# The meta tokens' attention gathered by key head, and four changes of order and engine at the borders of stages, in a two-layer attention and mLSTM trunk

## The chip, the cores and the metric

The kernel runs on one core of a Trainium2 chip, as one launch. A core has TensorE (PE, matrix products, with a weight load PEld of its own), VectorE (DVE), ScalarE (ACT), GpSimd (POOL) and SyncE (SP), which here only issues DMAs. The metric is the device time of one execution in microseconds (us), the median of several runs.

## The reference

Two layers; each normalises the rows, projects them once, runs two mixers side by side, gates both and projects back onto the residual. Sixteen learned meta rows stand ahead of the 1024 rows of x, and are dropped at the end. The first mixer is attention with 16 query heads on 2 key heads (8 query heads for each), a window of 128, the 16 meta keys always visible, and a sink logit for each head. The second is an mLSTM with 4 heads.

```python
h = concatenate([meta, x])                                   # 16 + 1024 rows of 1024
for l in range(2):
    z = rms_norm(h, norm_g) @ w_in
    aq, ak, av, ag, mq, mk, mv, mi, mf, mo, mgate = split(z)
    q, k = rope(rms_norm(aq, q_norm_g)), rope(rms_norm(ak, k_norm_g))
    # scores against 16 meta keys and the last 128 keys; the sink is one more term of the sum
    m = maximum(scores.max(-1), sink)
    e = exp(scores - m)
    probs = e / (e.sum(-1) + exp(sink - m))
    ya = (probs @ v) * silu(ag)
    qk = silu(causal_depthwise_conv(concatenate([mq, mk])))
    hm = rms_norm(mlstm(qk, mv, log_i, log_f), out_norm_g)
    ym = hm * sigmoid(mo) * silu(mgate)
    h = h + concatenate([ya, ym]) @ w_out
return h[16:]
```

A meta row's query sees only the meta keys that are not behind it, and the sink. Only layer 0 needs the outputs of the meta rows; in layer 1 they are dropped.

## The kernel before

All tensors are kept in float32. A product is made of two or three passes with each factor split into a rounded part (hi) and the rest (lo): ACT copies hi, then DVE or POOL subtracts. Rows are tiles t = 0 (the 16 meta rows) and t = 1 to 8 (128 rows each).

A layer runs as these stages: norm and key/value projection (`kv_tasks`), the first query projection (`q_tasks`), the attention over eight head pairs j, the mLSTM over four heads, and the output projection in four groups g (half of the tiles by half of the columns). `weave` interleaves a foreground list, the projection for a later stage, with a background list, the steps of attention or mLSTM. The matmuls stand on PE in the order of this code (`pin`); the instructions of the other engines are put in order by a scheduler that goes by readiness and priority, and `tc.high_priority(offset=EARLY)` moves some forward.

*Attention.* `att_tasks` gives, for a head pair j (two query heads, key head kv = j // 4), one step for each row tile b, in four parts that the background runs two and three steps apart. `s1`: the scores of tile b into bank S (L692), mask, maximum, exponentials, normalisation; in some steps ("visits") transposed queries ride in S's free columns (L633). `s2`: the probabilities are transposed into bank T (L738 for the 16 meta keys, L741 for the window), and evacuated to `HL` (L745, L748) and `pm` (L746, L749). `s3` and `s4`: the products with the values into bank O (L766, L778), evacuated by L781 and L783, multiplied by the gate G on POOL (L785) and stored to `spool` by SP. There are two S banks, one T and one O. In layer 0 b runs from 0 to 8 (`first_q` = 0), so each head pair has a ninth step, b = 0, with 16 query rows; its queries are turned by `q_meta` (L646) one head pair ahead. In layer 1 b runs from 1 to 8.

*Before the attention,* `q_tasks(0)` is the foreground. At its places n0+6 and n0+15 the keys of key head 0 are turned and stacked: `k_turn`, `k_stacks` (hi on ACT L444, lo on DVE L445) and `v_stacks` (ACT L452, POOL L453), for the first and the second half of the rows. `q_stacks` (L625, L610) turns the first queries.

*Elsewhere:* `fold` (L201, L202) adds the two halves of the product of the 16 meta rows. In the mLSTM, `sb` makes the factor of the output norm for each head and tile, 68 in all: DVE L1025 to L1029, a power on POOL (L1030), a DVE product (L1031), scaling on ACT (L1033), then a transpose on PE (L957). In the output projection `wout` splits a weight block on ACT (L185) and on POOL or DVE (L186), `y_split` splits a mixer's output (L1217, L1222), `product` is L1260, and `result` adds the residual (L1276, L1277) and takes squares (L1286). In group g = 2 of layer 0 the next layer's norm runs along: `norm_pre` (L291 to L295) and `norm_half` (L303 transposes, L307, L308).

Of the kernel before, what the change touches and what calls it, by code (L numbers as in the profile page):

```python
# [23 lines left out]
NEG = -1e30  # L24
# [12 lines left out]
WHEN = {0: (3, 4, 5, 6), 3: (2, 3, 4, 5), 4: (3, 4, 6, 7)}  # L37
FIRST = ((0, 0), (0, 1), (1, 0))


def _tables():
# [10 lines left out]
    cst = np.zeros((128, 166), f)  # L52
    cst[:, 0:128] = np.eye(128, dtype=f)
    cst[:, 128:164] = -0.5
    for r in range(64):
        cst[r, 164 + r // 16 % 2] = 1.0
    return {
# [7 lines left out]
def build(ctx, tc, I, O):  # L65
# [112 lines left out]
    def wout(l, k, c0, i, after=None):  # L178
# [7 lines left out]
        (ve if i > 8 and i % 2 else gp).tensor_tensor(lo, raw, hi, op=ALU.subtract)  # L186
# [11 lines left out]
    def fold(ps, n):  # L198

        a = w1k()  # L200
        sc.activation(a[:16, :n], ps[32:48, :n], AF.Copy)  # L201
        ve.tensor_tensor(a[:16, :n], ps[:16, :n], a[:16, :n], op=ALU.add)  # L202
        return a
# [169 lines left out]
    for l in range(DEPTH):  # L373
# [5 lines left out]
        AV = unit(F32R)[:, 0:896].rearrange("p (t c) -> p t c", t=7)  # L379
        DV = unit(F32R)[:, 0:896].rearrange("p (t c) -> p t c", t=7)  # L380
# [3 lines left out]
        KT = unit()[:, :].rearrange("p (a c) -> p a c", a=8)  # L384
        SS = []
# [87 lines left out]
        def kv_tasks():  # L473
# [13 lines left out]
            if l == 0:  # L487
# [4 lines left out]
                sy.dma_start(cst, I["cst"])  # L492
# [151 lines left out]
        def q_meta_turn(j, ps):  # L644
            c0 = 128 * (j % 2)
            pin(pe.transpose(ps, A[j]["q"]["XM"][:, c0:c0 + 128], ident[:16, :16]))  # L646
# [30 lines left out]
        def att_tasks(j, st):  # L677
# [3 lines left out]
            def s1(b):  # L681
# [21 lines left out]
                if b == 0:  # L703
                    ve.memset(band[:p], NEG)
                    mk = mask[:p, 128:144].bitcast(U32).rearrange("p (a c) -> p a c", a=1).to_broadcast([p, 2, 16])
                    ve.copy_predicated(cols(S, 130, 510, 16)[:p], mk,
                                       neg[:p].rearrange("p (a c) -> p a c", a=1).to_broadcast([p, 2, 16]))
# [18 lines left out]
                if meta:  # L726
                    q_put(q_unit(j + 1, 0)[:, 1024:1056], S[:, 0, 384:400], 16)
                live[b] = P

            def s2(b):  # L730
# [3 lines left out]
                HL = OW = None  # L734
# [4 lines left out]
                if b > 0:  # L739
                    for h in range(2):  # L740
# [626 lines left out]
```

## Time and profile before

| what | value |
|---|---|
| time, median of 3 runs (lowest to highest) | 1934.89 us (1934.46 to 1937.74) |
| the profiled execution | 1933.47 us |
| its span in the trace | 1931.7 us |
| granted TensorE clock | 1.00 |

The profile is one execution. Its rows give start, duration, engine, line, output <- input, shape; a number in square brackets is the idle time before the instruction and what ended it. A group's row has its count, then, behind a bar, the busy time of the engine in that group (overlaps counted once) and the mean duration of one instruction. The window rows give the window, its length, then busy time and count for PE, PEld, DVE, ACT and POOL, the granted clock, the DMAs' share and GB/s. A matmul's shape is contraction rows * output rows, then output rows x columns.

### The profile page before, as it was taken

Reading aid. Unit: us, or ns where it says so; the run is one execution under the profiler, and the core shown is the slowest. Engines: PE = TensorE matmul, PEld = TensorE weight load, DVE = VectorE, ACT = ScalarE, POOL = GpSimd, SP = SyncE. Lnnn points to the kernel's source line nnn. Section 1 sums busy time; section 2 is a strip of 40 time slices with the busy share of each in tenths; the row PEclk is TensorE's granted clock in tenths of the full one; section 3 lists DMA queues with packets and bytes.
Section 4 is the critical chain, followed back from the end, with each engine's and each line's share of the span. In section 5 each row is a group of like instructions: output and inputs, shape, how many; then the busy total and the mean of one; then the engine's idle time right before and its main releaser. Section 6 shows DMA issues by size and latency. Waiting matters only on the chain.

```text
span 1931.7 us, 36274 instructions
## 1 busy us (share of the span) xinstructions
PE 1902.6 (98%) x12827; PEld 1796.5 (93%) x12827; DVE 1051.2 (54%) x2914; ACT 1065.0 (55%) x3193; POOL 988.7 (51%) x1278
## 2 busy tenths in 40 slices
PE   8999999999999999999999999999999999999999
PEld 7999999999999999977789999999999999998887
DVE  7666766667354453542545667666573635437211
ACT  6577777746454554643334778776564545446221
POOL 3665756346545454564325467564465543647332
PEclk9999999999999999999999999999999999999999
DMA  4111111121222121554541111112122121216543
GB/s 155 32 45 40 38 44 43 45 65 41 64 54 59 43 62 50 154 170 159 176 134 36 44 48 38 49 48 60 40 59 64 47 71 41 62 59 195 167 148 125
DMA packets 150839, 148.28 MB, mean 77 GB/s; under 512 B 15081, under 2 KB 123921, under 8 KB 150658
## 3 DMA queue, kind: packets, MB, share of 16 engines
q1 hardware_dynamic: 150658, 145.97, 25.8%
q8 instruction: 101, 1.65, 0.4%
q14 instruction: 80, 0.66, 0.1%
HBM read 122.58 MB, written 23.29 MB: 76 GB/s over the span
## 4 chain that ended last, share of the span: by engine, by line
PE 82%; DVE 5%; ACT 3%; DMA 3%; POOL 3%; issue 2%; SPq 0%; ACTq 0%; POOLq 0%; DVEq 0%
PE pj L194 32%; PE pj L234 19%; PE pss L1260 6%; PE pj L1260 5%; PE po L1260 4%; PE S L692 3%; PE O L778 3%; PE po L957 2%; PE pss L957 2%; PE O L766 2%; PE T L741 1%; DMA raw<-in_w_out_dram 1%; DVE t L903 1%; PE pt L957 1%; PE pj L218 1%
## 5 line engine op out<-in xcount | busy, mean ns | idle before, releaser
L194 PE MATMUL pj<-H,RING 128*128 128x384 f32 (+2 forms) x3312 | 559.3, 322 | 0.0
L194 PEld LDWEIGHTS pj<-H,RING 128*128 128x128 f32 x3312 | 521.5, 188 | 2.3 <-issue 0.2
L168 POOL TENSOR_TENSOR RING<-raw,RING 128x512 fp32r<-128x512 f32 (+1 forms) x192 | 256.8, 1343 | 107.3 <-ACT RING L167 100.3
L234 PE MATMUL pj<-RING,H 128*128 128x256 f32 (+1 forms) x1920 | 268.8, 286 | 0.0
L234 PEld LDWEIGHTS pj<-RING,H 128*128 128x128 f32 x1920 | 242.2, 189 | 0.5
L234 PE MATMUL pj<-H,RING 128*128 128x384 f32 (+2 forms) x1296 | 239.7, 325 | 0.0
L186 POOL TENSOR_TENSOR RING<-raw,RING 128x512 fp32r<-128x512 f32 x96 | 126.1, 1320 | 172.8 <-ACT RING L185 159.7
L194 PE MATMUL pj<-RING,H 128*128 128x256 f32 x1536 | 209.6, 287 | 4.0 <-DVE w1k L202 2.1
L234 PEld LDWEIGHTS pj<-H,RING 128*128 128x128 f32 x1296 | 200.9, 188 | 0.1
L194 PEld LDWEIGHTS pj<-RING,H 128*128 128x128 f32 x1536 | 193.7, 191 | 6.5 <-DVE w1k L202 2.5
L185 ACT ACTIVATE RING<-raw 128x512 fp32r<-128x512 f32 x128 | 80.6, 631 | 174.8 <-DMA raw<-in_w_out_dram 155.4
L167 ACT ACTIVATE RING<-raw 128x512 fp32r<-128x512 f32 (+1 forms) x196 | 122.2, 625 | 47.0 <-DMA raw<-in_w_in_dram 35.2
L970 POOL TENSOR_TENSOR p<-u,p 128x258 fp32r<-128x258 f32 x64 | 49.5, 774 | 172.9 <-ACT p L969 164.9
L718 ACT ACTIVATE t<-S,mx 128x145 f32<-128x145 f32 (+1 forms) x272 | 99.4, 368 | 43.9 <-DVE mx L715 35.3
L785 POOL TENSOR_TENSOR u<-u,w1k 128x128 f32<-128x128 f32 (+1 forms) x136 | 61.9, 455 | 118.0 <-DVE w1k L783 102.2
L1260 PE MATMUL pss<-RING,H 128*128 128x512 f32 x384 | 120.5, 394 | 0.0
L756 POOL TENSOR_SCALAR_AFFINE_SELECT p<-p 128x512 fp32r<-128x512 f32 x112 | 71.4, 637 | 86.7 <-DVE p L748 85.7
L1260 PE MATMUL pj<-RING,H 128*128 128x512 f32 x352 | 110.3, 395 | 0.0
L903 DVE SCALAR_TENSOR_TENSOR t<-u,cw,t 128x384 f32<-128x384 f32 (+1 forms) x144 | 107.6, 747 | 2.0
L723 ACT ACTIVATE t<-t,mx 128x144 f32<-128x144 f32 (+1 forms) x272 | 97.7, 407 | 7.1 <-DVE mx L720 6.5
L926 DVE SCALAR_TENSOR_TENSOR t<-t,pj 128x384 f32<-128x384 f32 (+2 forms) x48 | 24.5, 511 | 124.9 <-ACT t L925 124.9
L1260 PE MATMUL po<-RING,H 128*128 128x512 f32 x288 | 91.3, 398 | 0.0
(347 smaller groups left out, 3841.3 us busy)
## 6 DMA issues: line engine op xcount, KB each, us to landing
raw<-in_w_out_dram SPq DMA_DIRECT2D x128, 256.0 KB, 2.8
raw<-in_w_in_dram SPq DMA_DIRECT2D x100, 256.0 KB, 2.8
raw<-in_w_in_dram SPq DMA_DIRECT2D x192, 128.0 KB, 2.3
spool<-u SPq DMA_DIRECT2D x56, 192.0 KB, 1.9
p<-x SPq DMA_DIRECT2D x24, 256.0 KB, 4.2
t<-spool SPq DMA_DIRECT2D x30, 192.0 KB, 3.6
p<-spool SPq DMA_DIRECT2D x26, 192.0 KB, 3.6
u<-em SPq DMA_DIRECT2D x8, 576.0 KB, 6.6
```

What stands on the lines that cost most here:

```text
L167: sc.activation(hi, raw[:, :, 0:o], AF.Copy)
L168: eng.tensor_tensor(lo, raw[:, :, 0:o], hi, op=ALU.subtract)
L185: sc.activation(hi, raw, AF.Copy)
L186: (ve if i > 8 and i % 2 else gp).tensor_tensor(lo, raw, hi, op=ALU.subtract)
L194: last = pin(pe.matmul(out, a, b, start=(i == 0), stop=(i == n - 1)))
L234: pin(pe.matmul(out(), x, y, start=(k + i == 0), stop=(k == n - 1 and i == 2)))
L718: sc.activation(P[:p, 145 * h:145 * h + 145], S[:p, h, 1 + 127 * h:146 + 127 * h], AF.Exp, bias=mx[:p, 0, h:h + 1], accum_out=mx[:p, 1, h: ...
L723: sc.activation(Pn, Pn, AF.Copy, scale=mx[:p, 2, h:h + 1])
L756: gp.affine_select(OW, HL, [[0, 4], [1, 128]], ALU.is_ge, 0.0, base=0, channel_multiplier=-1)
L903: ve.scalar_tensor_tensor(z, RAW[:, t0 + i:t0 + i + n], wcol(i), z, ALU.mult, ALU.add)
L957: pin(f(*a, **k))
L1260: pin(pe.matmul(ps[:p, :], a, b, start=(i + n == 0), stop=(i == 15 and n == len(terms) - 1)))
```

## The change

Five things are changed.

1. The meta queries' attention. The steps b = 0 of layer 0 are gone. The 16 queries of all eight heads of one key head are stacked to 128 columns (`QM`), and the steps named in `MRIDE`, b = 4 of j = 3 and of j = 7, carry them along: two score matmuls into free columns of S, `meta_probs`, one more transpose into T, one product into free columns of O, and `meta_out`, which multiplies by the gate's first 16 columns (kept in `GM`) and stores to `spool`. The queries are turned before the stage and in step b = 6 of j = 1, 3 and 5. `meta_consts` loads the mask and the sinks by nine small DMAs in the first head pair.
2. `fold`'s two operations get the higher priority.
3. `k_stacks` and `v_stacks` of the second half of the rows are called in the first head pair of the attention, not at n0+15.
4. In `sb` the product after the power goes from DVE to POOL; the constant factor is multiplied in by a DVE operation ahead of the power.
5. In group g = 2 of layer 0's output projection all weight splits go to DVE; before, they alternated between POOL and DVE from the ninth on.

```diff
+MRIDE = ((3, 4), (7, 4))
...
-    def wout(l, k, c0, i, after=None):
+    def wout(l, k, c0, i, after=None, eng=None):
...
-        (ve if i > 8 and i % 2 else gp).tensor_tensor(lo, raw, hi, op=ALU.subtract)
+        (eng or (ve if i > 8 and i % 2 else gp)).tensor_tensor(lo, raw, hi, op=ALU.subtract)
...
     def fold(ps, n):
 
         a = w1k()
-        sc.activation(a[:16, :n], ps[32:48, :n], AF.Copy)
-        ve.tensor_tensor(a[:16, :n], ps[:16, :n], a[:16, :n], op=ALU.add)
+        with tc.high_priority(offset=EARLY):
+            sc.activation(a[:16, :n], ps[32:48, :n], AF.Copy)
+            ve.tensor_tensor(a[:16, :n], ps[:16, :n], a[:16, :n], op=ALU.add)
         return a
...
+        AV, DV = unit(F32R), unit(F32R)
+        QMF, pmm = AV[:, 896:1152], DV[:, 896:1024]
+        QM = QMF.rearrange("p (v a h t) -> p v h a t", v=2, a=4, h=2)
+        AV, DV = [x[:, 0:896].rearrange("p (t c) -> p t c", t=7) for x in (AV, DV)]
...
-        def q_meta_turn(j, ps):
-            c0 = 128 * (j % 2)
-            pin(pe.transpose(ps, A[j]["q"]["XM"][:, c0:c0 + 128], ident[:16, :16]))
-
-        def q_meta(j, ps):
-
-            q_meta_turn(j, ps)
-            q_put(q_unit(j, 0)[:, 1024:1056], ps, 16)
+        def q_meta_turn(m, ps):
+            for i in range(2):
+                pin(pe.transpose(ps[:, i], QQ[m]["XM"][:, 128 * i:128 * i + 128], ident[:16, :16]))
+
+        def q_meta_put(m, src):
+
+            Q = QM[:, m // 2, :, 2 * (m % 2):2 * (m % 2) + 2]
+            sc.activation(Q[0:64, 0], src[0:64], AF.Copy)
+            sc.activation(Q[64:128, 1], src[64:128], AF.Copy)
+            ve.tensor_tensor(Q[64:128, 0], src[0:64], Q[0:64, 0], op=ALU.subtract)
+            ve.tensor_tensor(Q[0:64, 1], src[64:128], Q[64:128, 1], op=ALU.subtract)
+
+        def meta_probs(S, kv):
+
+            X = S[:, 0, 384:401]
+            one = lambda x: x.rearrange("p (a c) -> p a c", a=1)
+            ve.copy_predicated(one(X[:, 0:16]), one(mcst[:, 32:48].bitcast(U32)), one(neg).to_broadcast([128, 1, 16]))
+            ve.tensor_copy(X[:, 16:17], mcst[:, 48 + kv:49 + kv])
+            P, mx = mcst[:, 0:17], mcst[:, 20:23]
+            ve.tensor_reduce(mx[:, 0:1], X, axis=mybir.AxisListType.X, op=ALU.max, negate=True)
+            sc.activation(P, X, AF.Exp, bias=mx[:, 0:1], accum_out=mx[:, 1:2])
+            ve.reciprocal(mx[:, 2:3], mx[:, 1:2])
+            sc.activation(P[:, 0:16], P[:, 0:16], AF.Copy, scale=mx[:, 2:3])
+            return P
+
+        def meta_out(O, kv):
+
+            O = O[:, 256:384]
+            up, y = w1k(), w1k()
+            sc.activation(up[0:64, 0:128], O[64:128], AF.Copy)
+            y4 = y[:, 0:64].rearrange("p (a t) -> p a t", a=4)
+            o, u = [x[0:64, 0:128].rearrange("p (a h t) -> p h a t", a=4, h=2) for x in (O, up)]
+            for h in range(2):
+                ve.tensor_tensor(y4[64 * h:64 * h + 64], o[:, h], u[:, h], op=ALU.add)
+            gp.tensor_tensor(y4, y4, GM[:, 4 * kv:4 * kv + 4], op=ALU.mult)
+            sy.dma_start(spool[4 * kv:4 * kv + 4, :, 0:16].rearrange("j p t -> p j t"), y4)
...
+                    if a == 0:
+                        gp.tensor_copy(GM[:, j], st["G"][:, 0:16])
...
-                meta = b == 6 and j < 7 and first_q == 0
+                meta = b == 6 and j in (1, 3, 5) and not last
                 if meta:
-                    q_meta_turn(j + 1, S[:, 0, 384:400])
+                    q_meta_turn((j + 1) // 2, S[:, :, 384:400])
+                if (j, b) in MRIDE and not last:
+                    for i in range(2):
+                        pin(pe.matmul(S[:, 0, 384:400], QMF[:, 128 * kv:128 * kv + 128], Ks[i][:, 0:16], start=(i == 0), stop=(i == 1)))
...
-                if b == 0:
-                    ve.memset(band[:p], NEG)
-                    mk = mask[:p, 128:144].bitcast(U32).rearrange("p (a c) -> p a c", a=1).to_broadcast([p, 2, 16])
-                    ve.copy_predicated(cols(S, 130, 510, 16)[:p], mk,
-                                       neg[:p].rearrange("p (a c) -> p a c", a=1).to_broadcast([p, 2, 16]))
-                else:
-                    if b == 1:
-                        ve.memset(cols(S, 2, 510, 128), NEG)
-                    ve.copy_predicated(band, mask.bitcast(U32).rearrange("p (h c) -> p h c", h=2),
-                                       cols(S, 146, 366, 128))
+                if b == 1:
+                    ve.memset(cols(S, 2, 510, 128), NEG)
+                ve.copy_predicated(band, mask.bitcast(U32).rearrange("p (h c) -> p h c", h=2), cols(S, 146, 366, 128))
...
+                if (j, b) in MRIDE and not last:
+                    live["M"] = meta_probs(S, kv)
...
+                pmeta = live.pop("M") if (j, b) in MRIDE and not last else None
+                if pmeta is not None:
+                    tmm = X[0:16, 384:512]
+                    pin(pe.transpose(tmm, pmeta[:, 0:16], ident))
...
+                    if pmeta is not None:
+                        sc.activation(pmm[0:16], tmm, AF.Copy)
+                        ve.tensor_tensor(pmm[32:48], tmm, pmm[0:16], op=ALU.subtract)
...
+                mo = live.pop("O")
+                ride = (j, b) in MRIDE and not last
+                if ride:
+                    pin(pe.matmul(mo[:, 256:384], VM[:, kv, 0, :], pmm, start=True, stop=True))
...
+                    if ride:
+                        meta_out(mo, kv)
...
-                        a = N_META if (t0 == 0 and last) else t0
+                        a = t0 or N_META
                         sy.dma_start(spool[j, :, a:t0 + n], G[:, a:t0 + n])
...
-            return [(b, s1, s2, s3, s4) for b in range(first_q, 9)]
+            return [(b, s1, s2, s3, s4) for b in range(1, 9)]
...
                 ve.tensor_scalar(s4[:p, 1:2], s4[:p, 1:2], MV * EPS, None, ALU.add)
+                ve.tensor_scalar(s4[:p, 3:4], s4[:p, 0:1], math.sqrt(MV) * 0.25, None, ALU.mult)
                 gp.tensor_tensor(s4[:p, 2:3], s4[:p, 1:2], nhalf[:p, 0:1], op=ALU.pow)
-                ve.tensor_scalar(s4[:p, 2:3], s4[:p, 2:3], s4[:p, 0:1], math.sqrt(MV) * 0.25,
-                                 ALU.mult, ALU.mult)
+                gp.tensor_tensor(s4[:p, 2:3], s4[:p, 2:3], s4[:p, 3:4], op=ALU.mult)
                 sc.activation(num[:p, 0:256], num[:p, 0:256], AF.Copy, scale=s4[:p, 2:3])
...
+        def meta_consts():
+
+            sy.dma_start(mcst[:, 32:48], I["cst"][:, 166:182])
+            s0 = I["attn_sink"][l]
+            for h in range(8):
+                sy.dma_start(mcst[16 * h:16 * h + 16, 48:50],
+                             bass.AP(tensor=s0.tensor, offset=s0.offset + h, ap=[[0, 16], [8, 2]]))
...
+        def meta_first():
+            ps = bank("po")[:, 0:32].rearrange("p (a t) -> p a t", a=2)
+            q_meta_turn(0, ps)
+            q_meta_put(0, ps)
...
-              n0 + 15: [lambda: k_turn(1), lambda: (k_stacks(0, 1, 0), k_stacks(0, 1, 1)), lambda: v_stacks(0, 1)],
-              n0 + 21: [lambda: q_stacks(0, 0, "pss")] + ([lambda: q_meta(0, bank("po")[:, 0:16])] if first_q == 0 else [])}
+              n0 + 15: [lambda: k_turn(1)],
+              n0 + 21: [lambda: q_stacks(0, 0, "pss")] + ([] if last else [meta_first])}
...
+            if j == 0 and not last:
+                at.setdefault(14, []).append(meta_consts)
+            if j == 0:
+                for i, x in enumerate((lambda: k_stacks(0, 1, 0), lambda: k_stacks(0, 1, 1), lambda: v_stacks(0, 1))):
+                    at.setdefault(2 * i, []).append(x)
...
-                w = front.pop(0) if front else wout(l, order[i], c0, i)
+                w = front.pop(0) if front else wout(l, order[i], c0, i, None, ve if g == 2 and not last else None)
```

How the instructions stand, at three places. First PE in layer 0's attention, where head pair 1 begins. Before (L218 is a projection of the meta rows, L692 the scores, L738 and L741 the transposes, L766 and L778 the products, L234 the foreground):

```order
L778 MATMUL O<-p_1471,u 128x256 x2
L218 MATMUL pj<-RING,HM 48x256 x16
L692 MATMUL S_1050<-u 16x16 x4
L234 MATMUL pj<-RING,H 128x256 x6
L738 MATMUL T<-cst,t 32x128
L741 MATMUL T<-cst,t 128x128 x2
L234 MATMUL pj<-RING,H 128x256 x9
L766 MATMUL O<-p_1521,u 128x256 x2
L778 MATMUL O<-ptm_105,VM 128x128 x2
L778 MATMUL O<-p_1526,u 128x256 x2
L234 MATMUL pj<-RING,H 128x256 x9
L692 MATMUL S_1049<-u 128x144 x4
```

And in the changed kernel, whose lines are its own (L221 for L218, L731 for L692, L642 for L633, L237 for L234, L775 and L777 for L738 and L741, L806 and L818 for L766 and L778):

```order
L818 MATMUL O<-p_1451,u 128x256 x2
L221 MATMUL pj<-RING,HM 48x256 x16
L731 MATMUL S_1041<-u 128x144 x4
L642 MATMUL S_1041<-cst,u 128x128 x2
L237 MATMUL pj<-RING,H 128x256 x6
L775 MATMUL T<-cst,t 32x128
L777 MATMUL T<-cst,t 128x128 x2
L237 MATMUL pj<-RING,H 128x256 x9
L806 MATMUL O<-p_1502,u 128x256 x2
```

The scores of the meta rows (16x16) are gone, and the first full step of the head pair follows at once.

Second, POOL at the end of layer 1's mLSTM, at the last of the 68 powers (L1030). L1222 is `y_split`, L186 a weight split. Before:

```order
L186 TENSOR_TENSOR RING<-raw,RING 128x512
L1222 TENSOR_TENSOR u<-t,H 128x256
L1222 TENSOR_TENSOR u<-p_22915,H 128x384
L1030 TENSOR_TENSOR s_22694<-s_22694,cst 128x1
L1222 TENSOR_TENSOR u<-t,H 128x384
L186 TENSOR_TENSOR RING<-raw,RING 128x512
```

In the changed kernel (L1077 is the power, L1078 the new product, L1286 `y_split`, L188 the weight split):

```order
L188 TENSOR_TENSOR RING<-raw,RING 128x512
L1077 TENSOR_TENSOR s_22585<-s_22585,cst 128x1
L1286 TENSOR_TENSOR u<-t,H 128x256
L1286 TENSOR_TENSOR u<-p_22807,H 128x384
L1078 TENSOR_TENSOR s_22585<-s_22585 128x1
L1286 TENSOR_TENSOR u<-t,H 128x384
L188 TENSOR_TENSOR RING<-raw,RING 128x512
```

The power now stands ahead of two of POOL's splits and the product behind them. On PE the two transposes that need the result have 694 output-projection matmuls behind them, 689 before.

Third, DVE in layer 0's output projection, where the results of group 1 are taken out of their banks (L1276, L1277). Before:

```order
L1222 TENSOR_TENSOR u<-p_11657,H 128x384
L1222 TENSOR_TENSOR u<-p_11749,H 128x384
L186 TENSOR_TENSOR RING<-raw,RING 128x512 x4
L1276 TENSOR_TENSOR p_11771<-po,p_11771 16x512
L1277 TENSOR_TENSOR p_11771<-po,p_11771 16x512
```

In the changed kernel (L188 is L186, L1340 and L1341 are L1276 and L1277):

```order
L1286 TENSOR_TENSOR u<-p_11517,H 128x384
L1286 TENSOR_TENSOR u<-p_11609,H 128x384
L188 TENSOR_TENSOR RING<-raw,RING 128x512 x9
L1340 TENSOR_TENSOR p_11631<-po,p_11631 16x512
L1341 TENSOR_TENSOR p_11631<-po,p_11631 16x512
```

Nine weight splits stand ahead of the first result, where four stood. The order of PE and ACT is the same there. Where the second halves of the keys are stacked, DVE has the same rows in the same places in both kernels, in both layers: the normalised queries (L549), the two L445, then the rotation (L559, L563, L564). fold's two operations, too, stand behind the same rows as before at the two places where PE waits for them.

More of the change, by code (lines that the diff above doesn't have):

```diff
@@ L51, in _tables @@
     k = np.arange(128)[None, :]
-    cst = np.zeros((128, 166), f)
+    cst = np.zeros((128, 182), f)
     cst[:, 0:128] = np.eye(128, dtype=f)
@@ L56, in _tables @@
         cst[r, 164 + r // 16 % 2] = 1.0
+    cst[:, 166:182] = np.arange(16)[None, :] > np.arange(128)[:, None] % 16
     return {
@@ L384, in build @@
         KT = unit()[:, :].rearrange("p (a c) -> p a c", a=8)
+        GM = VR[:, 0].rearrange("p (j t) -> p j t", j=8)
+        mcst = KR[:, 0]
         SS = []
@@ L491, in kv_tasks @@
                 xt = {1: load_tile(1)}
-                sy.dma_start(cst, I["cst"])
+                sy.dma_start(cst, I["cst"][:, 0:166])
                 one = gr[0:1, D:D + 128]
@@ L519, in kv_tasks @@
                 ve.tensor_scalar(VM[:, i // 2, i % 2, :], ident, 0.0, None, ALU.mult)
+            if not last:
+                ve.tensor_scalar(pmm, ident, 0.0, None, ALU.mult)
             for i, t in enumerate(ts):
@@ L685, in s1 @@
                 blk[0] += 1
-                k0, kn, o = (0, 16, 128) if b == 0 else (0, 144, 128) if b == 1 else (16 + (b - 2) * 144, 272, 0)
+                k0, kn, o = (0, 144, 128) if b == 1 else (16 + (b - 2) * 144, 272, 0)
                 for h in range(2):
@@ L689, in s1 @@
                     i = (b - 1) % 4
-                    lq = U[:, 1024 + 16 * h:1040 + 16 * h] if b == 0 else U[:, 512 * h + 128 * i:512 * h + 128 * i + 128]
+                    lq = U[:, 512 * h + 128 * i:512 * h + 128 * i + 128]
                     for i in range(2):
@@ L733, in s2 @@
                 X = bank("T")
-                HL = OW = None
+                OW = None
                 pm = ptm[blk[1] % 2]
@@ L738, in s2 @@
                 pin(pe.transpose(tm, P[:p, 129:161], ident[:p, :p]))
-                if b > 0:
-                    for h in range(2):
-                        pin(pe.transpose(X[:, 128 * h:128 * h + 128], P[:, 1 + 160 * h:129 + 160 * h], ident))
+                for h in range(2):
+                    pin(pe.transpose(X[:, 128 * h:128 * h + 128], P[:, 1 + 160 * h:129 + 160 * h], ident))
+                pmeta = live.pop("M") if (j, b) in MRIDE and not last else None
+                if pmeta is not None:
+                    tmm = X[0:16, 384:512]
+                    pin(pe.transpose(tmm, pmeta[:, 0:16], ident))
                 with tc.high_priority(offset=EARLY):
-                    if b > 0:
-                        HL = p512(F32R)
-                        sc.activation(HL[:, 0:256], X[:, 0:256], AF.Copy)
+                    HL = p512(F32R)
+                    sc.activation(HL[:, 0:256], X[:, 0:256], AF.Copy)
                     taken = sc.activation(pm[0:32, 0:p], tm, AF.Copy).ins
-                    if b > 0:
-                        ve.tensor_tensor(HL[:, 256:512], X[:, 0:256], HL[:, 0:256], op=ALU.subtract)
+                    ve.tensor_tensor(HL[:, 256:512], X[:, 0:256], HL[:, 0:256], op=ALU.subtract)
                     ve.tensor_tensor(pm[32:64, 0:p], tm, pm[0:32, 0:p], op=ALU.subtract)
+                    if pmeta is not None:
+                        sc.activation(pmm[0:16], tmm, AF.Copy)
+                        ve.tensor_tensor(pmm[32:48], tmm, pmm[0:16], op=ALU.subtract)
                     w = splits.pop((j, b), None)
@@ L761, in s3 @@
                 pm, HL, OW = live.pop(b)
-                O = bank("O")
-                O = O[:, 0:256]
-                if b > 0:
-                    for i in range(2):
-                        pin(pe.matmul(O, AV[:, max(b - 2, 0)], HL[:, 256 * i:256 * i + 256], start=(i == 0), stop=False))
+                live["O"] = bank("O")
+                O = live["O"][:, 0:256]
+                for i in range(2):
+                    pin(pe.matmul(O, AV[:, max(b - 2, 0)], HL[:, 256 * i:256 * i + 256], start=(i == 0), stop=False))
                 live[b] = pm, OW, O
@@ L777, in s4 @@
                 for i, (V, R, o) in enumerate(prods):
-                    pin(pe.matmul(o, V, R, start=(b == 0), stop=(b == 0 or i == len(prods) - 1)))
+                    pin(pe.matmul(o, V, R, start=False, stop=(i == len(prods) - 1)))
+                mo = live.pop("O")
+                ride = (j, b) in MRIDE and not last
+                if ride:
+                    pin(pe.matmul(mo[:, 256:384], VM[:, kv, 0, :], pmm, start=True, stop=True))
                 up, y = w1k(), w1k()
@@ L1119, in build @@
         ns = len(steps) // 8
-        visits = {j * ns + 4 * g + i + 1 - first_q - 2: (j, g, i)
+        visits = {j * ns + 4 * g + i - 2: (j, g, i)
                   for j in range(8) for g in range(2) for i in (0, 2) if j + g > 0}
```

4 lines of the change are left out of this document (1 added, 3 removed).

## The prediction

> **What bounds the kernel now.** The page's head and first part say which engine sets the time: the span, and the busy time of each engine.
>
> ```profile
> span 1931.7 us, 36274 instructions
> PE 1902.6 (98%) x12827; PEld 1796.5 (93%) x12827; DVE 1051.2 (54%) x2914; ACT 1065.0 (55%) x3193; POOL 988.7 (51%) x1278
> ```
>
> TensorE (PE) is busy 98% of the span and no other engine above 55%. So time falls in two ways only: PE gets fewer matmuls, or it waits less. An edit on another engine is worth what PE waits for it. The windows show where PE waits; the two rows are the attention of layer 0 and of layer 1, which differ in the code only by the meta tokens' queries and their gate columns.
>
> ```profile
> 77.00:387.00 310.00, 302.17 (x2325) 294.35 (x2325) 210.26 (x664) 232.71 (x816) 177.01 (x279) 1.00 0.15 42
> 1057.00:1340.00 283.00, 282.82 (x2210) 280.60 (x2209) 192.78 (x585) 209.89 (x727) 166.15 (x249) 1.00 0.16 45
> ```
>
> PE idles 7.83 us in the first and 0.18 in the second; the granted clock is 1.00 in both. The timeline gives the borders: the first matmul of each stage and the first of the convolution after it.
>
> ```profile
> 76.70 0.66 PE L234 MATMUL pj<-H,RING 128*128 128x272 f32 x4
> 386.65 0.54 PE L234 MATMUL pj<-H,RING 128*128 128x272 f32 x3
> 1056.76 0.63 PE L234 MATMUL pj<-H,RING 128*128 128x256 f32 x4
> 1340.30 0.54 PE L234 MATMUL pj<-H,RING 128*128 128x272 f32 x3
> ```
>
> Layer 0 takes 386.65 - 76.70 = **309.95 us**, layer 1 1340.30 - 1056.76 = **283.54**. The 26.41 between them is the largest thing that this change can reach. The waits of PE and of its weight load (PEld) name the rest: total, times, longest.
>
> ```profile
> PE O L766 <- DVE w1k L783: 2.5, 6, 0.7
> PE pj L194 <- DVE w1k L202: 2.1, 2, 1.1
> PE pss L625 <- DVE u L564: 2.0, 2, 1.8
> PE pt L957 <- ACT w1k L1033: 1.3, 1, 1.3
> PEld O L766 <- ACT ptm L746: 6.3, 6, 1.7
> ```
>
> **Part A, the meta queries.** Which matmuls does layer 0 have that layer 1 lacks? These are the groups of the first window by shape, with layer 1's row of the gate projection (128x256) fourth; behind the bar is the time in which the group kept PE busy.
>
> ```profile
> L218 PE MATMUL pj<-RING,HM 128*48 128x256 f32 x48 | 6.1, 279 | 0.0
> L234 PE MATMUL pj<-H,RING 128*128 128x272 f32 x194 | 28.8, 292 | 0.0
> L234 PE MATMUL pj<-H,RING 128*128 128x256 f32 x192 | 27.5, 287 | 0.0
> L778 PE MATMUL O<-ptm,VM 128*128 128x16 f32 x16 | 2.3, 215 | 0.0
> L692 PE MATMUL S<-u 128*16 128x16 f32 x32 | 2.0, 171 | 0.0
> L646 PE MATMUL S<-cst,w1k 16*128 16x16 f32 x7 | 1.6, 230 | 0.0
> L738 PE MATMUL T<-cst,t 16*32 16x16 f32 x8 | 1.5, 187 | 0.0
> L738 PE MATMUL T<-cst,t 128*32 128x128 f32 x62 | 16.9, 272 | 0.0
> ```
>
> The 48 projections of the meta rows (6.1) and the 16 more gate columns (28.8 - 27.5, less two extra matmuls of 0.15, about 1.0) stay. The meta steps' own matmuls, 2.3 + 2.0 + 1.6 + 1.5 = 7.4, go. So 26.41 - 6.1 - 1.0 - 7.4 = 11.9 us are waiting that only layer 0 has. One of these waits, from the timeline:
>
> ```profile
> 233.26 0.25 ACT L746 ACTIVATE ptm<-T 32x128 fp32r<-32x128 f32 x1
> 233.43 0.23 DVE L706 COPY_PREDICATED_SCALAR S<-mask,neg 16x32 f32 x1
> 233.63 0.30 PEld L766 LDWEIGHTS O<-p,u 128*128 128x128 f32 x2 [1.66 <-ACT ptm L746]
> ```
>
> The meta step is a step like any other for VectorE (DVE) and ScalarE (ACT): mask, maximum, exponentials, sum, though 16 rows wide. On PE it is short, so the eight steps before and after it come closer together than DVE and ACT can evacuate their banks. With 64 steps in place of 72 this goes, and PE's order in layer 0 becomes layer 1's order of before, plus the L218 groups and the rides. Layer 1 runs that order with 0.18 idle.
>
> What is added on PE: six turns of 16x128 (by L646, 0.23 each: 1.4), four score matmuls and two products (by L778 128x16, 0.14: 0.8), two transposes (by L738 128x128, 0.27: 0.5). That is 2.7; as records overlap their neighbours, I take 2.0. On DVE and ACT each of the two rides adds about a meta step's work (seven DVE and four ACT operations of a small tile); its GpSimd (POOL) product and its store follow with nobody waiting soon. Eight meta steps cost 11.9 in waits, so one costs 1.5: two rides cost 3.0 at worst and nothing at best. I take 1.0, since PE's own work around them is not shortened.
>
> Layer 0 after: 283.54 + 6.1 + 1.0 + 2.0 + 1.0 = 293.6, that is **-16.3**. Bounds: -18.3 without waits at the rides and with half of the 2.0; -4.7 (7.4 - 2.7) if all waiting stays, and -1.7 with the rides' 3.0 on top. The nine small loads on SP stand in the first head pair, where the weights' loads have a whole step to land; nothing is waited for, 0. Zeroing pmm is one more DVE operation at the start, where PE waits anyhow; with the reordered start I put **+0.2** (0 to 0.5).
>
> **Parts B and C, fold and the key stacks.** In the window before layer 0's attention DVE has
>
> ```profile
> 70.63 1.51 DVE L445 TENSOR_TENSOR u<-u 64x576 fp32r<-64x576 f32 x2
> 73.22 0.44 PE L625 MATMUL pss<-cst,u 128*128 128x128 f32 x2 [1.76 <-DVE u L564]
> ```
>
> The two L445, queued ahead of L559 and L564, delay them by 1.51, and PE waits 1.76. Moving the call should free that. But the order of the built kernel has them on DVE at the very same place, between L549 and L559, in both layers: only PE's order follows the code. So the move does nothing, **0**. Likewise fold's two operations (2.1 in the list above) stand behind the same DVE rows as before: **0**. If either did work it would give up to 2.0 and 2.1.
>
> **Part D, the factor of the output norm.** Rows: shortest, median and longest duration, and the one place where PE waits.
>
> ```profile
> L1030 POOL TENSOR_TENSOR s<-s,cst x68: 538/550/918, 437.2 to 1763.1; 128x1 f32<-128x1 f32 x64, 16x1 f32<-16x1 f32 x4
> L1031 DVE TENSOR_SCALAR s<-s x68: 195/214/217, 438.0 to 1766.8; 128x1 f32<-128x1 f32 x64, 16x1 f32<-16x1 f32 x4
> 1760.22 1.05 POOL L1222 TENSOR_TENSOR u<-t,H 128x256 fp32r<-128x256 f32 x1
> 1761.74 1.36 POOL L1222 TENSOR_TENSOR u<-p,H 128x384 fp32r<-128x384 f32 x1 [0.47 <-ACT H L1217]
> 1763.06 0.73 POOL L1030 TENSOR_TENSOR s<-s,cst 128x1 f32<-128x1 f32 x1
> 1766.84 0.20 DVE L1031 TENSOR_SCALAR s<-s 128x1 f32<-128x1 f32 x1
> ```
>
> The power was ready at 1763.79, and the factor 3 us later, since L1031 stood behind DVE's splits. After, the product is POOL's: about 0.55, the price of the nearest POOL row of this shape, in place of 0.21. At this place the order puts two of POOL's splits (1.0 and 1.4 us) between power and product, the power ahead of both, and the transposes that wait stand five matmuls earlier from the end. So the power runs near 1761.7, the product ends near 1764.9, the scaling near 1765.6, and PE wants it near 1765.0: 0.6 of the wait of 1.3 to 1.5 stays, **-0.8**. Elsewhere no matmul waited for L1033, so the other 67 are put at 0. Bounds for all 68: -1.5 to +1.5, as PE's order moves by a few matmuls in the whole mLSTM.
>
> **Part E, the splits of the third output group.** PE waits there (windows 800 to 1010), and a DVE operation runs long beside a POOL split:
>
> ```profile
> PE pt L303 <- ACT pt L1286: 1.4, 1, 1.4
> PE pt L303 <- DVE H L308: 1.2, 2, 1.0
> 916.82 0.88 DVE L295 SCALAR_TENSOR_TENSOR p<-p,nv,w1k 128x256 f32<-128x256 f32 x2 [2.81 <-DMA p<-x]
> 949.02 1.92 DVE L295 SCALAR_TENSOR_TENSOR p<-p,nv,w1k 128x256 f32<-128x256 f32 x2
> 929.00 0.69 DVE L186 TENSOR_TENSOR RING<-raw,RING 128x512 fp32r<-128x512 f32 x1 [3.77 <-ACT RING L185]
> 949.20 1.45 POOL L186 TENSOR_TENSOR RING<-raw,RING 128x512 fp32r<-128x512 f32 x1 [1.44 <-ACT RING L185]
> 897.20 0.68 DVE L1276 TENSOR_TENSOR p<-po,p 16x512 f32<-16x512 f32 x1 [8.38 <-PE po L1260]
> 906.04 0.63 PE L1260 MATMUL po<-RING,H 128*128 128x512 f32 x2
> ```
>
> The pair of L295 takes 0.88 alone and 1.92 beside POOL: 1.04 goes with POOL's split, and the last wait (1.4) ends behind that pair. The other two (1.2) end at L308, behind such pairs and behind copies of weights whose buffers come free sooner with a split of 0.69 for 1.45; I take half, 0.6. That is **-1.6** of 2.6. Against it, nine DVE splits now stand ahead of L1276, where four stood. Each follows ACT's copy, so L1276 slips from 897.2 to about 902; its bank is wanted at 906.04, so it is hidden with some 3 us left. Were one more copy waited for, it would slip by 3 more: +1.0. Bounds -2.6 to +1.0.
>
> [...]
>
> **Sum.** -16.3 + 0.2 + 0 + 0 - 0.8 - 1.6 = -18.5. The profiled execution took 1933.47 (span 1931.7 and 1.8 around it): 1915.0. The median of the runs is 1934.89, 1.4 above it, so **1916.4**.
>
> **Rivals.** *The waits are the pipeline's own.* There is one T and one O bank, and each step's chain (scores, softmax, transposes, copies, product) may be the limit with or without meta steps. Then part A gives 4.7, the whole 4.7 - 0.2 + 0.8 + 1.6 = 6.9, time 1928.0. For it: the PEld row names the T bank's copy. Against: layer 1 runs 64 such chains and idles 0.18. Chance 0.14, parts of it counted.
> *POOL's product on the path (slower).* Place: the 68 factors of the mLSTM, 387 to 800 and 1340 to 1768. POOL's queue is in order; a product behind a split costs 1.3 to 1.5 more, and its own 0.55 stands for 0.21. Without part D the change gives 17.7; to lose that and 3.9 more, 21.6 / 68 = 0.32 us of each must reach PE. At 0.34, the difference of the two durations, the time is 1934.89 - 17.7 + 23 = 1940. For it: products adjacent to their power still wait for POOL's longer instruction. Against: PE waited for one L1033 in 68. Chance 0.03.
> *The moves of B and C act after all* (the change, as built, doesn't do there what it says, which is my forecast): 4.1 more, 1912.3. Against: DVE's rows. Chance 0.05.
> *Part E turns into a wait:* +1.0 for -1.6, 1919. Chance 0.08, inside the range.
>
> **Numbers.** The forecast holds 0.70 on 1910 to 1922. The low end takes part A at -18.3, E at -2.6 and D at -1.5, with 4.1 for B and C: 1908. The high end goes half way into the first rival, 1922.2, and adds most of a bad E: 1924. About 0.2% (3.9 us) is what a measurement can tell from no change: under 1931 is faster, 0.92; 1931 to 1938.8 is the same, 0.05, from the first rival with a bad E and part of the second; slower 0.03.
>
> **What would show it.** Right: the distance of the two borders in layer 0 falls to 292 to 295, PE's idle time there under 1.5, the rows before O L766 are gone or at the rides alone; L445 still before L559 and 1.8 before L625 again; L1031's wait at the end near 0.6; the L295 pairs near 0.88. Wrong: waits before L766 spread over the stage as before, or new waits of L957 for the POOL product.

## The result

The changed kernel takes 1913.07 us (median of 4 runs, 1912.79 to 1913.58), the kernel before 1935.17 (median of 4) beside it: a ratio of 0.9887, interval [0.9874, 0.9899], or 22.1 us less. The forecast was 1916.4 in 1908 to 1924. Against the one profiled execution of before (1933.47, span 1931.7) the profiled one of the changed kernel took 1913.58, span 1911.9: 19.9 less, where the sum said 18.5.

The head and first part of the changed kernel's page:

```profile
span 1911.9 us, 36057 instructions
PE 1892.1 (99%) x12779; PEld 1791.3 (94%) x12779; DVE 1035.6 (54%) x2876; ACT 1052.5 (55%) x3131; POOL 984.5 (51%) x1337
```

PE lost 10.5 us of busy time and 48 matmuls; the other half of the gain is idle time of PE that is gone. Its timeline at the four borders of the two attention stages, the same matmuls as in the prediction (L237 is L234 of before):

```profile
75.10 0.41 PE L237 MATMUL pj<-H,RING 128*128 128x272 f32 x2
368.32 0.41 PE L237 MATMUL pj<-H,RING 128*128 128x272 f32 x2
1037.52 0.40 PE L237 MATMUL pj<-H,RING 128*128 128x256 f32 x2
1321.09 0.41 PE L237 MATMUL pj<-H,RING 128*128 128x272 f32 x2
```

Layer 0's attention takes 368.32 - 75.10 = 293.2 us (forecast 293.6), layer 1's 283.57, as before. With the start of the first and of the last matmul of each output projection as further borders, the whole span divides like this:

| stretch | before | after | difference | forecast |
|---|---|---|---|---|
| start, to layer 0's attention | 76.70 | 75.10 | -1.60 | +0.2 |
| layer 0's attention | 309.95 | 293.22 | -16.73 | -16.3 |
| layer 0's mLSTM | 413.67 | 414.82 | +1.15 | 0 |
| layer 0's output projection, layer 1's start | 256.45 | 254.38 | -2.07 | -1.6 |
| layer 1's attention | 283.54 | 283.57 | +0.03 | 0 |
| layer 1's mLSTM | 406.56 | 406.93 | +0.37 | 0 |
| layer 1's output projection | 180.73 | 179.63 | -1.10 | -0.8 |
| rest | 4.16 | 4.22 | +0.06 | 0 |

The two mLSTM rows are scatter: in the other three profiles of kernels that keep the meta steps, layer 0's mLSTM took 413.6 to 416.1 and layer 1's 405.8 to 406.6.

The windows of the two stages, and PE's waits in the first of them (75 to 368):

```profile
75.00:368.00 293.00, 292.52 (x2275) 289.44 (x2274) 197.95 (x613) 217.61 (x752) 177.08 (x281) 1.00 0.15 43
1037.00:1321.00 284.00, 283.81 (x2218) 281.59 (x2217) 193.80 (x588) 210.49 (x727) 167.43 (x250) 1.00 0.16 45
PE T L775 <- DVE u L790: 0.3, 1, 0.3
PE T L775 <- DVE ptm L787: 0.2, 1, 0.2
```

PE's idle time in layer 0's attention fell from 7.83 to 0.48, and no wait before the first product (L766, now L806) is left.

### The profile page after: what moved, and what is told of

Its sections match the earlier page's. It is cut to its first block, busy times and chain, and to the rows that moved or that the text cites. A ratio compares the mean times of both kernels' runs of the same rounds, so it can differ in the third digit from the quotient of the medians.

```text
span 1911.9 us, 36057 instructions
## 1 busy us (share of the span) xinstructions
PE 1892.1 (99%) x12779; PEld 1791.3 (94%) x12779; DVE 1035.6 (54%) x2876; ACT 1052.5 (55%) x3131; POOL 984.5 (51%) x1337
## 3 DMA queue, kind: packets, MB, share of 16 engines
q8 instruction: 101, 1.65, 0.4%
## 4 chain that ended last, share of the span: by engine, by line
PE 85%; DVE 4%; DMA 4%; issue 3%; POOL 3%; ACT 2%; SPq 0%; POOLq 0%; ACTq 0%; DVEq 0%
PE pj L196 32%; PE pj L237 22%; PE pss L1324 6%; PE pj L1324 4%; PE po L1324 4%; PE S L731 3%; PE O L818 3%; PE po L1003 2%; PE pss L1003 2%; DMA raw<-in_w_out_dram 2%; PE O L806 2%; PE T L777 1%; PE pj L221 1%; PE pt L1003 1%; DVE t L949 1%
## 5 line engine op out<-in xcount | busy, mean ns | idle before, releaser
L237 PE MATMUL pj<-RING,H 128*128 128x256 f32 (+1 forms) x1920 | 269.3, 286 | 0.3 <-ACT u L541 0.3
L237 PEld LDWEIGHTS pj<-RING,H 128*128 128x128 f32 x1920 | 242.4, 189 | 0.7 <-ACT u L541 0.6
L237 PE MATMUL pj<-H,RING 128*128 128x384 f32 (+2 forms) x1296 | 239.2, 324 | 0.0
L237 PEld LDWEIGHTS pj<-H,RING 128*128 128x128 f32 x1296 | 201.1, 188 | 0.0
L188 POOL TENSOR_TENSOR RING<-raw,RING 128x512 fp32r<-128x512 f32 x85 | 110.9, 1311 | 154.6 <-ACT RING L187 137.6
L753 ACT ACTIVATE t<-S,mx 128x145 f32<-128x145 f32 x256 | 93.6, 368 | 36.5 <-DVE mx L750 32.0
L831 POOL TENSOR_TENSOR u<-u,w1k 128x128 f32<-128x128 f32 x128 | 60.3, 471 | 92.2 <-DVE w1k L827 85.1
L188 DVE TENSOR_TENSOR RING<-raw,RING 128x512 fp32r<-128x512 f32 x43 | 34.6, 806 | 124.5 <-ACT RING L187 124.5
L758 ACT ACTIVATE t<-t,mx 128x144 f32<-128x144 f32 x256 | 91.9, 407 | 4.5 <-DVE mx L755 3.9
```

Source lines behind the costliest of these rows:

```text
L188: (eng or (ve if i > 8 and i % 2 else gp)).tensor_tensor(lo, raw, hi, op=ALU.subtract)
L237: pin(pe.matmul(out(), x, y, start=(k + i == 0), stop=(k == n - 1 and i == 2)))
L753: sc.activation(P[:p, 145 * h:145 * h + 145], S[:p, h, 1 + 127 * h:146 + 127 * h], AF.Exp, bias=mx[:p, 0, h:h + 1], accum_out=mx[:p, 1, h: ...
L758: sc.activation(Pn, Pn, AF.Copy, scale=mx[:p, 2, h:h + 1])
```

## The experiments

Stage times below are read at the same matmuls as in the table; "layer 0" and "layer 1" stand for their attention stages.

**Which part carries the gain.** Part A alone: the kernel before with `att_tasks` from b = 1, the rides and all that belongs to them, the other edits undone.

```diff
-            return [(b, s1, s2, s3, s4) for b in range(first_q, 9)]
+            return [(b, s1, s2, s3, s4) for b in range(1, 9)]
```

> Part A alone on the kernel before. If the gain of layer 0's attention belongs to part A alone: its borders 293 us apart as with the whole change (309.95 before), the whole about 16.5 to 17.5 us under the kernel before. If it needs the moved key stacks or the other parts: the borders over 296, the whole less than 14 under.

Layer 0 took 293.19; the whole 1918.01, ratio 0.9924 [0.9907, 0.9940], some 15 to 16 us under the kernel before. So the 16.7 belong to A, but alone it gives back about 2: its output projection of layer 0 took 258.73 instead of 256.45. The start was 74.57, so the gain there comes with A as well.

All but A: the kernel before with the edits of B to E.

```diff
-        sc.activation(a[:16, :n], ps[32:48, :n], AF.Copy)
+        with tc.high_priority(offset=EARLY):
+            sc.activation(a[:16, :n], ps[32:48, :n], AF.Copy)
...
+                gp.tensor_tensor(s4[:p, 2:3], s4[:p, 2:3], s4[:p, 3:4], op=ALU.mult)
...
+                w = front.pop(0) if front else wout(l, order[i], c0, i, None, ve if g == 2 and not last else None)
```

> Parts B to E on the kernel before, with the meta steps kept. If the parts add up: 3 to 4.5 us under the kernel before (22.1 less part A's 17 to 18), with layer 0's attention still near 310 us. If part A is worth more together with the others: 0 to 2 under.

1935.06, ratio 1.0005 [0.9995, 1.0014]: nothing. The expected 3 to 4.5 was a miss; the other branch, 0 to 2, holds at its low end. The parts do not add up: with the meta steps kept, the four small edits are worth nothing that can be measured.

**Part C, the moved stacks, alone.**

```diff
-              n0 + 15: [lambda: k_turn(1), lambda: (k_stacks(0, 1, 0), k_stacks(0, 1, 1)), lambda: v_stacks(0, 1)],
+              n0 + 15: [lambda: k_turn(1)],
...
+                for i, x in enumerate((lambda: k_stacks(0, 1, 0), lambda: k_stacks(0, 1, 1), lambda: v_stacks(0, 1))):
```

> Part C alone on the kernel before. The forecast's reading (the two DVE operations stay ahead of the rotation, so nothing moves): 0, PE's wait before L625 stays 1.8. Its rival (the value stacks leave POOL's queue and DVE's side, so that the second power starts 1.7 us sooner): the wait falls to about 0.5, the attention of layer 0 begins 1.3 to 1.6 us sooner, the whole 1 to 2 us under.

1.0002 [0.9992, 1.0011]: nothing, as forecast. The built kernel has the same instructions in the same order as before on PE, DVE and ACT, and on POOL one weight split a row or two earlier. That makes it a second profile of the kernel before, which the sections below use. Then why does L625 (now L634) wait 0.5 in place of 1.8 in the changed kernel? POOL's timeline ahead of the second power (L586, now L595), with some rows between left out, before:

```profile
63.57 0.72 POOL L453 TENSOR_TENSOR u<-u 128x256 fp32r<-128x256 f32 x1
64.26 1.04 POOL L453 TENSOR_TENSOR u<-w1k,u 128x192 fp32r<-128x192 f32 x1
65.27 0.58 POOL L453 TENSOR_TENSOR u<-u 128x192 fp32r<-128x192 f32 x1
65.82 0.73 POOL L453 TENSOR_TENSOR u<-w1k,u 128x256 fp32r<-128x256 f32 x1
68.00 0.24 POOL L585 TENSOR_SCALAR ssq__743<-ssq__743 128x8 f32<-128x8 f32 x1 [1.17 <-DVE ssq__743 L584]
68.32 1.67 POOL L586 TENSOR_TENSOR ssq__743<-ssq__743,cst 128x8 f32<-128x8 f32 x1
```

In the changed kernel:

```profile
63.30 1.73 POOL L460 TENSOR_TENSOR u<-u 128x256 fp32r<-128x256 f32 x2
65.00 0.46 POOL L568 TENSOR_TENSOR t<-w1k,qrt 16x32 f32<-16x32 f32 x2
66.66 1.66 POOL L595 TENSOR_TENSOR ssq__744<-ssq__744,cst 128x8 f32<-128x8 f32 x1
```

And DVE's rotation beside them with the sum of squares (L584, now L593) that the power needs, before and after; the last row is PE's wait in the changed kernel:

```profile
64.88 1.75 DVE L559 TENSOR_TENSOR t<-u,qrt 128x64 f32<-128x64 f32 x2
67.22 0.69 DVE L584 TENSOR_REDUCE ssq__743<-pj 128x8 f32<-128x512 f32 x1
```

```profile
64.61 0.71 DVE L568 TENSOR_TENSOR t<-u,qrt 128x64 f32<-128x64 f32 x2
65.57 0.68 DVE L593 TENSOR_REDUCE ssq__744<-pj 128x8 f32<-128x512 f32 x1
71.55 0.44 PE L634 MATMUL pss<-cst,u 128*128 128x128 f32 x2 [0.54 <-DVE u L573]
```

Four value splits (L453, now L460) stood there, now two; the other two run earlier. Before, POOL was idle for 1.17 ahead of the power and waited for DVE's sum. The rotation, beside two splits and not four, took 0.71 instead of 1.75, and the sum now stands ahead of the rotation's last step (L564, now L573). So the sum began 1.65 sooner and the power 1.66. The two L445 (now L452), to which the prediction laid PE's wait, still take 1.51 at the same place. That the overlap with the splits is what made the rotation long was read from the rows, not tested. Part A alone shows the same order and a wait of 0.6, so this is the scheduler's answer to the removed meta work.

**Why the waits of layer 0 go.** Is it the meta step's small work on DVE and ACT? The kernel before without that work: the meta rows' mask, maximum, exponentials and normalisation are left out, and a constant stands for their probabilities.

```diff
+                if b == 0:
+                    P = cst
+                else:
```

> The kernel before, its nine steps and PE's matmuls kept, but the meta step's mask, maximum, exponentials and normalisation on VectorE and ScalarE left out (a constant stands for its probabilities, so the meta rows' attention is not computed). If the waits before L766 come from that small work in the two engines' queues: layer 0's attention falls from 310 to 298 to 301 us, with few waits left. If they come from the step itself, short on PE and still turning over the single T and O banks: 306 to 310.

Layer 0 took 308.48, and its waits are still there:

```profile
PE O L769 <- DVE w1k L786: 5.8, 11, 1.1
PEld O L769 <- ACT t L726: 3.9, 5, 1.3
PEld O L769 <- ACT ptm L749: 3.6, 4, 1.1
```

(L769 is L766, L786 is L783, which empties bank O.) Of the 16.7 us, 1.5 were the small work, and 4.8 are matmuls: 7.4 went, and 2.6 came for turns and rides (293.2 less 283.5, 6.1 and 1.0). For the other 10.4 there is the spacing: nine steps share the 24 or so parts of a head pair's foreground that eight share in layer 1. Counted from the rows of PE, between a step's last product into O and the next step's first there stand only 6 foreground matmuls at five places of layer 0 before, and never fewer than 12 in layer 1 or in layer 0 of the changed kernel. If that is the cause, it must work in layer 1 too:

```diff
-            weave(fg, [x for i in range(j * ns, j * ns + ns) for x in step(i)])
+            items = [x for i in range(j * ns, j * ns + ns) for x in step(i)]
+            cut = len(fg) * 8 // 9 if last else len(fg)
+            weave(fg[:cut], items)
+            for f in fg[cut:]:
+                f()
```

> The changed kernel, but in layer 1's attention the foreground is woven with only eight ninths of its parts, and the last ninth of each head pair's runs behind its steps: the same work, with as few foreground matmuls between the parts of a step as layer 0 had with nine steps a head pair. If the waits of the kernel before came from that spacing: layer 1's attention rises from 283.5 to 288 to 296 us, with waits before the second product (L806). If they came from the meta step being short on PE: 283.5 to 285.

Layer 1 rose from 283.55 to 289.64, with the same work and these waits of PE (1038 to 1330; L827 is L783 of before):

```profile
PE O L806 <- DVE w1k L827: 3.6, 7, 1.0
PE T L775 <- DVE ptm L787: 0.2, 1, 0.2
```

Four places had 6 or 9 foreground matmuls there. So spacing alone can make 6.1 us of such waits; how the rest of layer 0's 11.9 divides between spacing and the meta step's shortness on PE was not tried.

**What a ride costs.** The changed kernel without rides (the meta rows' attention is not computed), and with each made twice:

```diff
-MRIDE = ((3, 4), (7, 4))
+MRIDE = ()
```

> The changed kernel without the two rides (the meta rows' attention is not computed; the queries are still turned). If a ride costs only its matmuls on PE: layer 0's attention 292.2 to 292.8 us instead of 293.2. If each also costs waits as a meta step did (1.5): 290 to 291.

```diff
-MRIDE = ((3, 4), (7, 4))
+MRIDE = ((2, 8), (3, 4), (6, 8), (7, 4))
```

> The changed kernel with every ride made twice (the second pair in step 8 of head pairs 2 and 6). If a ride costs only its matmuls: 293.6 to 294.2 us for layer 0's attention. If it costs waits: 295 to 296.5, with waits before the second product in those steps.

Layer 0 took 291.98 without, 293.21 with two, 294.84 with four: 1.2 for the first two and 1.6 for the next two, 0.6 to 0.8 for one. Both expectations were a little off: it is more than the matmuls alone and far from a wait of 1.5. The excess of the first two is a short wait, 0.3 in head pair 7 (the row L775 <- L790 above), gone without the rides. With four rides a wait of 0.4 before the first product (L806) is added; what else makes the next two dearer was not traced.

**Part D, the factor on POOL.** The changed kernel with the product on DVE again, run on two chips.

```diff
-                ve.tensor_scalar(s4[:p, 3:4], s4[:p, 0:1], math.sqrt(MV) * 0.25, None, ALU.mult)
...
-                gp.tensor_tensor(s4[:p, 2:3], s4[:p, 2:3], s4[:p, 3:4], op=ALU.mult)
+                ve.tensor_scalar(s4[:p, 2:3], s4[:p, 2:3], s4[:p, 0:1], math.sqrt(MV) * 0.25,
+                                 ALU.mult, ALU.mult)
```

> The changed kernel with part D undone (the product after the power on DVE again). If part D gives 1.1 at the end of layer 1 and costs the 1.5 by which the two mLSTM stages grew: 0.4 us under the changed kernel, stages back to 413.7 and 406.6 us, the wait before the last transposes back at 1.3 or more. If the growth comes from elsewhere: 1.1 over the changed kernel, with the stages as long as there.

> The changed kernel without part D, timed beside it. If D's added POOL work costs what the stages showed (0.5 in each mLSTM, 0.4 in the last projection): 1 to 1.5 us under the changed kernel. If that was scatter: the same within 0.8.

1912.86 (ratio 0.9891) the first time; the second 1913.54, beside 1914.53 for the changed kernel on that chip (ratios 0.9891 [0.9876, 0.9906] and 0.9897 [0.9882, 0.9912]). No difference can be told. The wait at the end, for which D was charged, is not a fixed cost of the kernel before: its second profile (part C alone) has, between 1700 and 1800,

```profile
PE pt L957 <- ACT w1k L1033: 0.2, 1, 0.2
```

where the first had 1.3. The new POOL product itself is short (shortest, median, longest):

```profile
L1078 POOL TENSOR_TENSOR s<-s x68: 184/195/644, 420.2 to 1744.8; 128x1 f32<-128x1 f32 x64, 16x1 f32<-16x1 f32 x4
```

**Part E, the splits.** The changed kernel with them on POOL and DVE by turns again.

```diff
-                w = front.pop(0) if front else wout(l, order[i], c0, i, None, ve if g == 2 and not last else None)
+                w = front.pop(0) if front else wout(l, order[i], c0, i)
```

> The changed kernel with part E undone (weight splits of the third group on POOL and VectorE by turns). If part E is worth what the forecast said: layer 0's output projection to layer 1's attention 256 us or more instead of 254.4, the whole 1.6 us or more over the changed kernel, and pairs of L295's operation near 1.9 us again. If its gain came from the shifted start of other work: 254 to 255.

1917.92, ratio 0.9911 [0.9894, 0.9928]. That is 4.9 us over the changed kernel's first median, against the same 1935.17 of before, and 2.7 by the ratio that the changed kernel had in its second timing (0.9897, below); the intervals of these ratios overlap, so the time alone would leave part E in doubt. The stage is clearer: layer 0's output projection took 261.18. The timeline shows one wait of PE and what leads to it:

```profile
913.70 1.27 POOL L188 TENSOR_TENSOR RING<-raw,RING 128x512 fp32r<-128x512 f32 x1 [3.38 <-ACT RING L187]
917.75 0.63 ACT L187 ACTIVATE RING<-raw 128x512 fp32r<-128x512 f32 x1 [2.70 <-DMA raw<-in_w_out_dram]
918.29 0.20 ACT L310 ACTIVATE H<-pt 128x64 fp32r<-128x64 f32 x1
918.52 0.22 DVE L311 TENSOR_TENSOR H<-pt,H 128x64 fp32r<-128x64 f32 x1 [2.75 <-ACT H L310]
918.81 0.47 PE L306 MATMUL pt<-cst,p 128*128 128x128 f32 x1 [4.73 <-DVE H L311]
```

The split ends at 914.97 and frees a weight buffer; the next block's DMA is issued, which lands 2.7 us later; ACT copies it; and only behind that copy in ACT's queue does L310 empty the bank that PE's transposes want. A split of 0.69 on DVE in place of 1.27 shortens every turn of this ring. In the changed kernel the place costs nothing. In all profiles with part A: the two without part E have this wait, 2.5 (A alone) and 4.7, and a stage of 258.73 and 261.18; of the eight with part E seven have none and one has 1.3, and their stage takes 253.0 to 256.9. Without part A the same edit gives nothing (256.83 with it, 256.45 and 256.97 without): there the ring met the transposes in another phase. But for part D's own rows, PE and DVE have the same order in this stage with and without A, so why A shifts that phase stays open.

**The parts that matter, alone**, beside the changed kernel on the same chip: A and E on the kernel before, B, C and D undone.

> The changed kernel once more, on the same chip as the next two: 1912 to 1914.5 us, 21 to 22 under the kernel before; layer 0's attention 293.2.

> Parts A and E alone on the kernel before. If B, C and D give nothing: the time of the changed kernel within 1.5 us, and layer 0's start within 0.7. If they carry the 2 to 3 us by which the forecast was short: 2 to 3 us over it.

1914.53 (1911.62 to 1917.14) and 1913.11 (1911.94 to 1914.76), ratios 0.9897 [0.9882, 0.9912] and 0.9890 [0.9873, 0.9906]. A and E are the change; B, C and D add nothing that can be told. Against A alone (0.9924 [0.9907, 0.9940], on another chip) the ratio of A and E is lower beyond both intervals.

## Why the prediction was right, and where it was not

- *Part A, -16.3: measured -16.73.* The reading of layer 1 as layer 0 without meta steps held: 293.22 for 293.6. The mechanism held in its main claim (steps too close for one O bank), and the tightened layer 1 shows that such spacing alone makes 6.1 of such waits; where the other 4.3 of the 10.4 come from stays open. The first rival, that the waits are the pipeline's own with or without meta steps, is refuted. The rides' waits were put at 1.0 and are near 0.3: PE is idle 0.48 in the stage with the rides and 0.18 without them. Of the 11.9 that the prediction calls waiting, PE's idle time shows 7.65 (7.83 less 0.18); the other 4.2 stood as busy time of PE's records, and where was not traced.
- *Start, +0.2: measured -1.60.* The step that failed is the one that gave A no effect there. The changed order of POOL's value splits and of DVE's sum moves the second power 1.7 us forward, and L625's wait falls by 1.2, to 0.54, against the sign "1.8 before L625 again". No price was put on the moved rows. The two L445, to which the prediction laid that wait, still stand in the chain with 1.51; what changed is when the chain ahead of them starts.
- *Part C, 0: right,* and for the reason given: alone, it leaves the order on DVE as it was. Part B was not run alone; with A and E in place and B, C and D undone the time is the same.
- *Part D, -0.8: nothing.* The stage ended 1.10 sooner in the profile, but D is not why: without it that stage took 179.2 and 179.5, with it 179.2 to 181.6 over the runs. So the nearness of 1.10 to 0.8 is luck. The term took one execution's wait for a constant. The product's price was also too high, 0.55 for a measured median of 0.195; the nearest row of the same shape was a power.
- *Part E, -1.6: -2.07 in the profile, and 2.7 to 4.9 beside the changed kernel without it.* The split of the term was wrong. It gave 1.0 to the last wait, which it laid to a pair of L295 beside a POOL split. In the rows that pair does not set it: the wait ends with the squares (L1286, now L1350) of a result (L1277, now L1341), and that result stands for the DMA of its row of x, in both kernels. 1.1 of the 1.4 is left:

```profile
951.84 0.69 DVE L1277 TENSOR_TENSOR p<-po,p 128x512 f32<-128x512 f32 x1 [0.31 <-DMA p<-in_x_dram]
932.08 0.69 DVE L1341 TENSOR_TENSOR p<-po,p 128x512 f32<-128x512 f32 x1 [0.35 <-DMA p<-in_x_dram]
PE pt L306 <- ACT pt L1350: 1.1, 1, 1.1
```

  The term gave 0.6 to the two waits at L308, half of their 1.2: these are gone whole. That the sum came out near is luck. The bank of L1276, its bound of +1.0, never waited.

- *The total is 3.6 us short against the medians:* 2.2 of that is the profiled executions, before's 1.7 faster than its median and the changed kernel's 0.5 slower than its own. The last section has a likely reason for most of the 1.7. The remaining 1.4 is the balance of the table, the start above all.
- *The slower rival* (POOL's product on the path) did not happen: with a median of 0.195 the product costs no more than DVE's 0.214.
- *The stretched pairs:* pairs of the norm's operation (L295, now L298) in the changed kernel, one alone and three of the late ones, the last with the split beside it:

```profile
898.14 0.88 DVE L298 SCALAR_TENSOR_TENSOR p<-p,nv,w1k 128x256 f32<-128x256 f32 x2 [0.60 <-DMA p<-x]
919.73 2.60 DVE L298 SCALAR_TENSOR_TENSOR p<-p,nv,w1k 128x256 f32<-128x256 f32 x2 [0.46 <-DMA p<-x]
923.97 1.92 DVE L298 SCALAR_TENSOR_TENSOR p<-p,nv,w1k 128x256 f32<-128x256 f32 x2 [1.04 <-DMA p<-x]
926.41 1.98 DVE L298 SCALAR_TENSOR_TENSOR p<-p,nv,w1k 128x256 f32<-128x256 f32 x2
926.42 1.30 POOL L188 TENSOR_TENSOR RING<-raw,RING 128x512 fp32r<-128x512 f32 x1 [0.81 <-ACT RING L187]
```

  The four early pairs of this shape run at 0.88, where three of four did before (the other took 1.69). The four late ones still meet POOL's splits of the next group: 2.60, 1.92, 1.98 and 1.28, for 2.72, 1.92, 1.93 and 1.92 before. So only one stretched pair of this shape went. In the two profiles the nine such pairs with a POOL split beside them take 1.28 to 2.72, the seven others 0.88.

## What to carry to other kernels

When two stages run the same program but for one block, the difference of their lengths, less the block's own work, is what the block costs in waits; here the forecast built on it was 16.3 for a measured 16.7. A short step in a pipeline like this one, with a single accumulator bank, can cost more than its work: here the stage fell by 16.7 us for 4.8 us less of matmuls, and fewer foreground matmuls between the products of neighbouring steps, by themselves, cost 6.1 us in layer 1. Gather such steps into riders on full ones, at 0.6 to 0.8 us each here. Take a wait of one execution as a sample, not a constant, and price every row that the scheduler moves, on the engines that the edit does not name too.

## What the runs showed of the hardware

After one wait of PE of 1.8 us the granted clock was lower in three of four executions, and in the fourth it was not. Four profiles have the same wait of 1.8 us before L625 at 71 to 74: the kernel before, part C alone, all but A, and the light meta step. Their windows right behind it, in this order:

```profile
74.00:78.00 4.00, 4.00 (x35) 4.00 (x35) 1.72 (x4) 2.33 (x6) 3.68 (x6) 1.00 0.00 0
74.00:78.00 4.00, 4.00 (x24) 4.00 (x25) 1.72 (x4) 1.31 (x4) 3.68 (x6) 0.64 0.00 0
74.00:78.00 4.00, 4.00 (x23) 4.00 (x22) 1.72 (x4) 1.18 (x4) 3.68 (x6) 0.57 0.00 0
74.00:78.00 4.00, 4.00 (x22) 3.96 (x22) 1.86 (x5) 1.54 (x4) 3.53 (x5) 0.59 0.00 0
```

The order on PE is the same, yet three of the four executions ran the next 4 us at 0.57 to 0.64 of the clock. At 0.64 that is 24 matmuls for 35, or 1.4 us lost (0.36 of the 4.00, an estimate). Layer 0's attention began at 76.70 in the first and at 78.06, 78.15 and 78.51 in the others. In the ten profiles in which this wait is 0.5 to 0.6, all with part A, the window has 1.00 and the attention begins at 74.55 to 75.10. So the -1.60 of the table compares with the one execution in which the clock held; against the other three the start gains about 3 us. This is the likely reason why the profiled execution of before was faster than its median; that the timed executions mostly lost the clock is not shown.

After the 4.73 us wait of the kernel with the old splits the clock was 0.52 for 6 us:

```profile
919.00:925.00 6.00, 6.00 (x18) 4.75 (x18) 4.26 (x15) 1.86 (x4) 0.84 (x2) 0.52 0.54 166
```

Ahead of the first transposes PE waited 1.97 in the kernel before (to 8.25, L303) and 2.29 in the changed kernel (to 8.41, L306), and there the clock stayed at 1.00. So the 1.8 us before L625 cost themselves and, in three of four executions, by the starts of the attention, some 1.4 to 1.8 us more.
